# Seven buffers for modulation pieces, state evictions of the scan on ScalarE, and more turns between a solve and its product

## The chip, the cores and the metric

The kernel runs on one core of one Trainium2 chip. The metric is the device time of one execution in microseconds; it is given as the median of several runs. A trace of one profiled execution belongs to it.

In the views, PE is TensorE (PEld its weight loads), DVE is VectorE, ACT is ScalarE, POOL is GpSimd and SP the SyncE queue. A name such as `L99` is line 99 of the kernel. All operations that go through the helper class `Paced` carry its line, L49, so they are told apart by the names of their tiles.

## The reference

The kernel computes one inference step of a hybrid decoder layer in float32, for a prompt of 512 tokens and 8 single-token samples:

```python
mod = silu(c) @ w_ada + b_ada
sh1, sc1, gt1, sh2, sc2, gt2 = split(mod, 6)
h = modulate(rmsnorm(x, g_norm_mix), sh1, sc1)
proj = h @ w_in                      # q, k, v | columns of the RWKV-7 mixer
att = banded_attention(q, k, v)      # window 128, ALiBi, sinks
rw, S = rwkv7_mix(p_rwkv, S0)        # S_t = S diag(w) + (S a) b^T + v k^T ; y_t = S_t r_t
x = x + gt1 * (concat(att, rw) @ w_out)
h2 = modulate(rmsnorm(x, g_norm_ffn), sh2, sc2)
gate, up = split(h2 @ w_ffn_in, 2)
x = x + gt2 * ((silu(gate) * up) @ w_ffn_out)
y = rmsnorm(x, g_norm_final)
```

The model width is 2048, and there are 16 RWKV heads of 64. The modulation matrix `w_ada` is 2048 by 12288.

## The kernel before, in words

Each large matrix product is done with float32 weights split into a high and a low part. `unit` (L82 to L93) loads 128 x 512 weights into a `raw` buffer over the SP queue, ScalarE rounds them to `wh` (L89), and VectorE takes the rest as `wl` (L92). `mm3` (L95) multiplies with three products of two halves of the tokens (260 columns each), so one unit of four k-steps is 24 matmuls. There are three buffers each of `raw`, `wh` and `wl`.

After the modulation of the first norm, the stage this change bears on runs: `rwkv_phase` (L483). TensorE computes the projection tiles of `w_in` (`pm`, L99). Beside them run generators, the background jobs: `pump` (called once per k-step, six projection matmuls) advances each job that is due by one turn, that is up to its next `yield`. The jobs are:

- `ada_gen` (L308): the remaining modulation columns. 64 groups of four pieces of `w_ada` are loaded by SP into four tiles of the tag `ar` (L315 to L317), and 16 small matmuls per group (L322) sum them into the PSUM tile `ada`. The tag `ar` has 5 buffers. It also serves `adar` (results of a column group), `sp` (attention projections on their way to DRAM, L468) and, in the FFN, `s3` (L1499).
- For each of eight head pairs: `rwkv_prep1`, `rwkv_prep2` and `rwkv_rest` (L707). `rwkv_rest` first solves 32 x 32 triangular systems on VectorE, in 31 steps of a product (`stmp`, L721) and a sum (`Tt`, L724). The solution goes through DRAM to be laid out again: four DMAs `TTd<-Tt` from POOL and SP (L731), then one DMA `Td<-TTd` from POOL (L732). VectorE copies `Td` into `TT`. After one turn TensorE multiplies `TT` with `L3` into `pu` (two products; `L3` prints as `L`), and ScalarE copies `pu` back.
- The scan of the pair follows, 16 steps, each a chain across engines: TensorE forms `psc<-Z,L`; ScalarE copies the result to `Z` (two copies of 32 x 64); TensorE forms `psc<-Z,LS`; VectorE multiplies the result by the decay column `PC` and writes it as the state of the next step into `Z` (two `tensor_scalar` of 64 x 64, L777). The last step writes to a piece of `L3` instead, for the output. The next step's `psc<-Z,L` waits for this.

The order of instructions on an engine is not the order of the code. The tile framework takes the instructions in the order of the code as priority, and at each point gives an engine the first of them that is ready by the framework's own estimate of durations. An instruction that isn't ready by that estimate is thus passed by later ones. Each engine then executes its queue strictly in the order so found, and waits where the estimate was too early. An SP or POOL DMA whose buffer isn't free holds up all later DMAs of its queue.

After the stage come attention, the output projection, the FFN (`ffn_in`, `ffn_out`) and the last norm. In `ffn_in` POOL issues DMAs that add to a tile in SBUF (L1500, L1503), one of them to `s3`.

Of the kernel before, what the change touches and what calls it, by code (L numbers as in the profile page):

```python
# [7 lines left out]
F32 = mybir.dt.float32  # L8
F32R = mybir.dt.float32r
AF = mybir.ActivationFunctionType  # L10
ALU = mybir.AluOpType
# [3 lines left out]
P = 128  # L15
# [48 lines left out]
class Kern:  # L64
# [194 lines left out]

    def ada_finish(self, f0, n, ps):  # L260
        nc = self.px
        res = self.w.tile([P, 512], F32, tag="ar", bufs=5, name=self.nm("adar"))
        nc.scalar.copy(res[:, :n * 128], ps[:, :n * 128])
        yield
        p2 = self.aux("adT")
        for f in range(n):
            nc.tensor.matmul(p2[:, f * 16:f * 16 + 9], res[:, f * 128:(f + 1) * 128], self.sel, start=True, stop=True)
        nc.vector.tensor_tensor(
            self.mod[:, f0:f0 + n, :],
            p2[:, :n * 16].rearrange("p (f t) -> p f t", f=n)[:, :, :9],  # L270
            self.par[:, P_BA + f0:P_BA + f0 + n].unsqueeze(2).broadcast_to([P, n, 9]),
            ALU.add,
        )
# [34 lines left out]
    def ada_gen(self):  # L308
        nc = self.px
        for c in (GT1, SH2, SC2, GT2):  # L310
            for q in range(4):
                ci = c // 4 + q
                ps = self.hold("ada")
                for k0 in range(0, KD, 4):
                    raws = [self.w.tile([P, 512], F32, tag="ar", bufs=5, name=self.nm("ar")) for _ in range(4)]  # L315
                    for k, raw in enumerate(raws, k0):
                        self.nc.sync.dma_start(raw, self.I["w_ada2"][ci - 8, k])  # L317
                    self.done_at += 2.5
                    yield
                    for k, raw in enumerate(raws, k0):  # L320
                        for j in range(4):
                            self.nc.tensor.matmul(  # L322
                                ps[32 * j:32 * j + 32, 0:128], self.cT[:, k, :], raw[:, j * 128:(j + 1) * 128],
                                start=k == 0, stop=k == KD - 1, tile_position=(0, 32 * j), skip_group_check=True,
                            )
                    self.spent(self.nc.tensor, 0.8)
                    yield
                    yield
                res = self.w.tile([P, 512], F32, tag="ar", bufs=5, name=self.nm("adar"))[:, 0:128]
                nc.scalar.copy(res, ps[:, 0:128])  # L330
                yield
                p2 = self.aux("adT")
                nc.tensor.transpose(p2[:, 0:128], res, self.ident)
                nc.vector.tensor_tensor(
                    self.mod[:, 4 * ci:4 * ci + 4, :], p2[:, 0:128].rearrange("p (f t) -> p f t", f=4)[:, :, 0:9],
                    self.par[:, P_BA + 4 * ci:P_BA + 4 * ci + 4].unsqueeze(2).broadcast_to([P, 4, 9]), ALU.add)
# [41 lines left out]
    def startup(self):  # L378
        nc, I = self.nc, self.I
        xs = self.x_tiles()  # L380
        c = self.w.tile([P, 512], F32, tag="ar", bufs=5, name=self.nm("cr"))[:, 0:144]
        nc.sync.dma_start(c, I["c"].rearrange("p k t -> p (k t)"))
        k = 0
        for t, n in xs:
            nc.sync.dma_start(t, I["x"][:, k:k + n])
            k += n
        xk = [t[:, i] for t, n in xs for i in range(n)]
        nc.vector.memset(self.cT[:, :, 9:32], 0.0)
        nc.scalar.activation(self.cT[:, :, 0:9], c.rearrange("p (k t) -> p k t", t=9), AF.Silu)
        nc.scalar.activation(c[:, 0:2], self.cT[:, 0, 0:2], AF.Square)  # L390
        nc.scalar.activation(c[:, 2:4], c[:, 0:2], AF.Sqrt)
        ps = self.ps_m.tile([P, 2, 512], F32, tag="m", name="ssq1")
        for k in range(0, KD, 2):
            sq = [self.t520(t) for t in (("tC", "tD"), ("tA", "tB"))[k // 2 % 2]]
            nc.scalar.activation(sq[0], xk[k], AF.Square)
            if k % 4:
                nc.vector.tensor_tensor(sq[1], xk[k + 1], xk[k + 1], ALU.mult)
            else:
                nc.scalar.activation(sq[1], xk[k + 1], AF.Square)
            nc.vector.tensor_tensor(sq[0], sq[0], sq[1], ALU.add)  # L400
            for h in range(2):
                nc.tensor.matmul(ps[:, h, :HB], self.ones, sq[0][:, h], start=k == 0, stop=k == KD - 2)
        rstd = self.rstd_of(self.t520("tF"), ps)
        self.pcs, self.ring, self.used = {}, [], set()
        head = []
        for idx in (I_WA, I_G0, I_G1, 8, 0):
            src, m = self.w_in_src(idx)
            head.append((src, m, self.new_pc(idx)[:m, 1:513], self.SC[:m, idx]))
        self.hk = 0
        self.start(self.seq(self.h_parts(xk, rstd), self.ada_gen()))  # L410
        for k0, k1 in ((0, 2), (2, 4), (4, 8), (8, 12), (12, 14), (14, 16)):
            while self.hk < k1:
                self.pump()
            for tile_ in head:
                self.part_tile(*tile_, k0, k1)
# [44 lines left out]
    def filler(self):  # L460

        if not self.spills:
            self.pump()
            return
        idx, dram, scols = self.spills.pop(0)
        nc = self.nc
        ps = self.main_tile(self.I["w_in"][idx], self.hH, self.hL)
        t = self.w.tile([P, 512], F32, tag="ar", bufs=5, name=self.nm("sp"))  # L468
        nc.scalar.copy(t.rearrange("p (h t) -> p h t", h=2), ps[:, :, 0:256])
        nc.vector.tensor_copy(scols, ps[:, :, 256:260])  # L470
        nc.sync.dma_start(dram, t)
# [235 lines left out]
    def rwkv_rest(self, d):  # L707
        nc, I, rc = self.px, self.I, self.rc
        hp, L3, PC = (d[n] for n in ("hp", "L3", "PC"))
# [25 lines left out]
        for c4 in range(4):  # L735
            ro = slice(32 * c4, 32 * c4 + 32)
            nc.vector.tensor_copy(TT[ro, :, 32 * c4:32 * c4 + 32], Td[ro])
        yield
        for e in range(2):
            pu = self.aux("pu")  # L740
            for cq in range(4):
# [19 lines left out]
        for c in range(16):  # L761
            ps = self.aux_c(hp % 2)
            for e, o in ((0, 96), (1, 64)):
                nc.tensor.matmul(ps[o:o + 32, 0:64], L3[:, e, c // 4, (c % 4) * 32:(c % 4) * 32 + 32], Z[:, c, e],
                                 start=True, stop=True, skip_group_check=True, tile_position=(0, o))
            for e, o in ((0, 96), (1, 64)):
                nc.scalar.copy(Z[96:128, c, e], ps[o:o + 32, 0:64])
            self.done_at = self.now() + 1.2
            yield
            dst = Z[0:64, c + 1] if c < 15 else SF  # L770
            for e in range(2):
                ro = slice(64 * e, 64 * e + 64)
                nc.tensor.matmul(ps[ro, 64:128], LS[:, e, c, :], Z[:, c, e], start=True, stop=True, skip_group_check=True,
                                 tile_position=(0, 64 * e))
            for e in range(2):
                ro = slice(64 * e, 64 * e + 64)
                nc.vector.tensor_scalar(dst[:, e], ps[ro, 64:128], PC[ro, c:c + 1], None, ALU.mult)  # L777
            self.done_at = self.now() + 1.2
            yield
        nc.gpsimd.dma_start(self.O["wkvp"][:, hp], SF)  # L780
# [633 lines left out]
    def ffn_in(self, st):  # L1414
# [3 lines left out]
        tc, nc, I = self.tc, self.nc, self.I  # L1418
# [9 lines left out]
        sp = self.fpb.enter_context(tc.tile_pool(name="strw", bufs=1))  # L1428
# [5 lines left out]
        def load(ht, row, col, g, tag="sr"):  # L1434
            pool, n = (self.w, 3) if tag == "raw" else (sp, 6)
            if tag in places:
                pool, (tag, n) = self.xp, tag
            t = pool.tile([P, 512], F32, tag=tag, bufs=n, name=self.nm(tag))
            nc.sync.dma_start(t, src(ht, row, col, g))
            return t  # L1440
# [31 lines left out]
        for ht in range(early):  # L1472
            ps = mt("pm")
# [13 lines left out]
        for i, ht in enumerate(order):  # L1487
# [7 lines left out]
            for g in range(2):  # L1495
                a11, a21 = load(ht, 0, 0, g), load(ht, 1, 0, g, places[(2 * i + g) % 4])
                a22 = load(ht, 1, 1, g, "raw")
                a12 = load(ht, 0, 1, g)
                s3 = self.w.tile([P, 512], F32, tag="ar", bufs=5, name=self.nm("s3"))  # L1499
                nc.gpsimd.dma_start(a21, src(ht, 1, 1, g), accum_op=ALU.add)  # L1500
                if not (old and g):
                    nc.sync.dma_start(s3, src(ht, 0, 0, g))
# [251 lines left out]
```

## Time and profile before

| what | value |
|---|---|
| median of 3 runs | 2674.15 us (2666.03 to 2679.41) |
| profiled execution, its own time | 2681.19 us |
| its span, first to last instruction | 2679.4 us |
| mean granted TensorE clock | 0.976 |
| busy: PE, DVE, ACT, POOL | 2549.8, 1717.3, 1085.4, 380.0 us |
| `ada_gen`'s matmuls | 140.1 to 712.1 us |
| scans' matmuls `psc<-Z,L` | 267.8 to 871.0 us |
| FFN, about | 1230 to 2679 us |

The profiled execution took 7 us more than the median of the runs. A sum of stalls is made against it and then carried to the median as a difference. TensorE is busy nearly all the time, so what counts is its idle time and what ended it; idle time of the other engines matters only where TensorE waits for them.

### The profile page before, as it was taken

The page shows a single profiled execution, that of the slowest core. Times are in us where ns is not written, and L with a number is a line of the kernel's source. Part 1 is how long each engine was busy: PE and PEld are TensorE (multiplying, and loading weights), DVE is VectorE, ACT ScalarE, POOL GpSimd, SP SyncE. Part 2 cuts the span into 40 slices and gives each one's busy share as a digit, 9 for nine tenths or more (in the row PEclk, how much of TensorE's full clock was granted, in tenths as well). Part 3 has the DMA queues.
Part 4 walks back from the last instruction along what each step waited for, and adds up shares of the span by engine and source line. Part 5 has one row for each costly group of instructions (what it writes and reads, how often), then busy time and mean ns, then how long its engine had stood idle before and what let it go on. Part 6 is the DMA issues. An engine that isn't in the chain of part 4 may idle for free. (4 is left out here: it accounts for less than half of the span.)

```text
span 2679.4 us, 59146 instructions
## 1 busy us (share of the span) xinstructions
PE 2549.8 (95%) x23373; PEld 2367.4 (88%) x23373; DVE 1717.3 (64%) x3883; ACT 1085.4 (41%) x2155; POOL 380.0 (14%) x532
## 2 busy tenths in 40 slices
PE   7898999999999899998999999999999999999997
PEld 4587877778788898898999999999999999999997
DVE  5466656677656744568877777777777763444456
ACT  3133335344333323547544444444444432222225
POOL 0011111121111120011111121121121100000003
PEclk9998999999999997999999999999999999999999
DMA  9865564655423474445677777777787562343333
GB/s 339 294 197 181 172 198 151 189 164 187 132 86 106 165 231 141 120 143 180 186 206 182 211 207 194 195 204 196 186 219 199 133 206 91 123 127 97 119 103 111
DMA packets 241702, 460.21 MB, mean 172 GB/s; under 512 B 32352, under 2 KB 44560, under 8 KB 241392
## 3 DMA queue, kind: packets, MB, share of 16 engines
q1 hardware_dynamic: 206160, 377.22, 43.1%
q0 software_dynamic: 34624, 78.16, 13.5%
q8 instruction: 183, 3.00, 0.5%
q10 hardware_dynamic: 640, 1.05, 0.1%
q14 instruction: 95, 0.78, 0.1%
HBM read 421.73 MB, written 35.59 MB: 171 GB/s over the span
## 5 line engine op out<-in xcount | busy, mean ns | idle before, releaser
L89 ACT CAST wh<-raw 128x512 fp32r<-128x512 f32 (+2 forms) x410 | 247.0, 606 | 544.9 <-PE pf L99 281.1
L92 DVE TENSOR_TENSOR wl<-raw,wh 128x512 fp32r<-128x512 f32 (+2 forms) x410 | 283.9, 695 | 211.0 <-ACT wh L89 206.7
L99 PE MATMUL pf<-go,wh 128*128 128x260 f32 x2560 | 414.1, 281 | 0.0
L99 PEld LDWEIGHTS pf<-go,wh 128*128 128x128 f32 x2560 | 353.9, 188 | 0.1
L1282 ACT CAST wh<-sr 128x512 fp32r<-128x512 f32 x320 | 198.1, 621 | 261.0 <-PE pm L1453 235.1
L99 PE MATMUL pm<-hH,wh 128*128 128x260 f32 (+1 forms) x1248 | 290.9, 311 | 8.6 <-ACT wh L89 7.5
L99 PE MATMUL pm<-hH,wl 128*128 128x260 f32 (+1 forms) x1248 | 267.0, 293 | 12.1 <-DVE wl L92 12.0
L1283 DVE TENSOR_TENSOR wl<-sr,wh 128x512 fp32r<-128x512 f32 x320 | 220.3, 689 | 83.1 <-ACT wh L1282 76.1
L99 PE MATMUL pf<-go,wl 128*128 128x260 f32 x1280 | 267.7, 282 | 0.0
L99 PE MATMUL pm<-hL,wh 128*128 128x260 f32 (+1 forms) x1248 | 267.7, 293 | 0.0
L1453 PE MATMUL pm<-xT,wh 128*128 128x260 f32 x1408 | 263.6, 286 | 2.9 <-DVE pc L1530 2.5
L1453 PE MATMUL pm<-T,wh 128*128 128x260 f32 x1408 | 257.6, 283 | 0.0
L99 PEld LDWEIGHTS pm<-hH,wh 128*128 128x128 f32 (+1 forms) x1248 | 198.6, 192 | 46.6 <-issue 22.9
L1453 PEld LDWEIGHTS pm<-xT,wh 128*128 128x128 f32 x1408 | 217.2, 189 | 9.5 <-DVE pc L1530 4.6
L99 PEld LDWEIGHTS pm<-hH,wl 128*128 128x128 f32 (+1 forms) x1248 | 197.9, 192 | 23.1 <-DVE wl L92 15.5
L1453 PEld LDWEIGHTS pm<-T,wh 128*128 128x128 f32 x1408 | 216.9, 188 | 0.0
L1453 PE MATMUL pm<-B0H,wl 128*128 128x260 f32 x704 | 200.8, 286 | 8.6 <-DVE wl L1283 8.4
L99 PEld LDWEIGHTS pm<-hL,wh 128*128 128x128 f32 (+1 forms) x1248 | 198.7, 192 | 7.6 <-issue 3.9
L1453 PE MATMUL pm<-B0H,wh 128*128 128x260 f32 x704 | 200.2, 284 | 2.7 <-DVE acct L1219 1.7
L99 PEld LDWEIGHTS pf<-go,wl 128*128 128x128 f32 x1280 | 200.9, 188 | 0.0
L1453 PE MATMUL pm<-B0L,wh 128*128 128x260 f32 x704 | 198.9, 283 | 0.0
L1453 PE MATMUL pm<-T,wl 128*128 128x260 f32 x704 | 198.7, 282 | 0.0
(426 smaller groups left out, 5254.0 us busy)
## 6 DMA issues: line engine op xcount, KB each, us to landing
ar<-in_w_ada SPq DMA_DIRECT2D x256, 256.0 KB, 3.9
sr<-in_w_fi SPq DMA_DIRECT2D x176, 256.0 KB, 4.3
raw<-in_w_fo SPq DMA_DIRECT2D x176, 256.0 KB, 2.6
raw<-in_w_in SPq DMA_DIRECT2D x144, 256.0 KB, 3.8
araw<-in_w_ada SPq DMA_DIRECT2D x64, 512.0 KB, 6.3
raw<-in_w_fi SPq DMA_DIRECT2D x120, 256.0 KB, 4.4
s<-in_w_fi SPq DMA_DIRECT2D x80, 256.0 KB, 4.8
s<-in_w_fi POOLq DMA_DIRECT2D x80, 256.0 KB, 5.5
```

What stands on the lines that cost most here:

```text
L89: nc.scalar.copy(wh[:, :n], raw[:, :n])
L92: nc.vector.tensor_tensor(wl[:, :n], raw[:, :n], wh[:, :n].bitcast(F32), ALU.subtract)
L99: nc.tensor.matmul(ps[:m, bank, :HB], w, a[:, k, h, :], start=first and i == 0, stop=last and i == 2, skip_group_check=True,)
L1282: nc.scalar.copy(H, src)
L1283: nc.vector.tensor_tensor(L, src, H.bitcast(F32), ALU.subtract)
L1453: nc.tensor.matmul(ps[:, :HB], x[:, s], y, start=g == k == i == 0, stop=g == 1 and k == 3 and i == 2, skip_group_check=True)
```

## The change

- The tag `ar` gets 7 buffers in place of 5, at all five places that name it. The 4 KiB per partition come out of the scratch in which POOL's DMA descriptors are kept, which goes from 8192 to 4096 bytes per partition.
- The two evictions at the end of each scan step (256 in all) become `activation` with the function Copy and the column `PC` as scale, on ScalarE.
- `rwkv_rest` yields four times in place of once between the copies into `TT` and the products `pu`.

```diff
-        res = self.w.tile([P, 512], F32, tag="ar", bufs=5, name=self.nm("adar"))
+        res = self.w.tile([P, 512], F32, tag="ar", bufs=7, name=self.nm("adar"))
...
-                    raws = [self.w.tile([P, 512], F32, tag="ar", bufs=5, name=self.nm("ar")) for _ in range(4)]
+                    raws = [self.w.tile([P, 512], F32, tag="ar", bufs=7, name=self.nm("ar")) for _ in range(4)]
...
             nc.vector.tensor_copy(TT[ro, :, 32 * c4:32 * c4 + 32], Td[ro])
-        yield
+        for _ in range(4):
+            yield
         for e in range(2):
             pu = self.aux("pu")
...
             for e in range(2):
                 ro = slice(64 * e, 64 * e + 64)
-                nc.vector.tensor_scalar(dst[:, e], ps[ro, 64:128], PC[ro, c:c + 1], None, ALU.mult)
+                nc.scalar.activation(dst[:, e], ps[ro, 64:128], AF.Copy, scale=PC[ro, c:c + 1])
...
-                s3 = self.w.tile([P, 512], F32, tag="ar", bufs=5, name=self.nm("s3"))
+                s3 = self.w.tile([P, 512], F32, tag="ar", bufs=7, name=self.nm("s3"))
...
-    nc = bacc.Bacc("TRN2", target_bir_lowering=False, num_devices=1, dynamic_dma_scratch_size=8192)
+    nc = bacc.Bacc("TRN2", target_bir_lowering=False, num_devices=1, dynamic_dma_scratch_size=4096)
```

The line numbers after the `yield` are one higher in the changed kernel. The order of the queues changes as follows.

TensorE's queue at the first pair's product `pu`, before. `pm` are projection tiles, `wh` and `wl` the weights of a unit, `ada` the modulation sums from pieces `ar`, `pV` the first product behind `pu`:

```order
L99 MATMUL pm_2755<-hH,wl_2968 128x260 x2
L322 MATMUL ada_2861<-ar_2957,cT 32x128 x4
L322 MATMUL ada_2861<-ar_2958,cT 32x128 x4
L322 MATMUL ada_2861<-ar_2959,cT 32x128 x4
L322 MATMUL ada_2861<-ar_2960,cT 32x128 x4
L99 MATMUL pm_2755<-hH,wh_2967 128x260 x2
L99 MATMUL pm_2755<-hL,wh_2967 128x260 x2
L99 MATMUL pm_2755<-hH,wl_2968 128x260 x2
L99 MATMUL pm_3030<-hH,wh_3033 128x260 x2
L49 MATMUL pu_2904<-TT,L_288_1790 128x128 x4
L49 MATMUL pu_2939<-TT,L_288_1790 128x128 x4
L49 MATMUL pV_2985<-cst,V_2259 128x128 x4
```

The same place in the changed kernel:

```order
L99 MATMUL pm_2755<-hH,wh_2953 128x260 x2
L99 MATMUL pm_2755<-hL,wh_2953 128x260 x2
L99 MATMUL pm_2755<-hH,wl_2954 128x260 x2
L322 MATMUL ada_2861<-ar_2969,cT 32x128 x4
L322 MATMUL ada_2861<-ar_2970,cT 32x128 x4
L322 MATMUL ada_2861<-ar_2971,cT 32x128 x4
L322 MATMUL ada_2861<-ar_2972,cT 32x128 x4
L99 MATMUL pm_3028<-hH,wh_3031 128x260
L49 MATMUL pu_2945<-TT,L_288_1790 128x128 x4
L49 MATMUL pu_2977<-TT,L_288_1790 128x128 x4
L49 MATMUL pV_3014<-cst,V_2259 128x128 x4
```

The product stands at the same weight unit's start as before, one projection matmul into it in place of two; ahead of it there are 961 projection matmuls in the whole queue, and 962 before. The modulation group moved to stand right in front of it. Numbers of tiles grow in the order of the code: `pu_2904` is written ahead of the units 2967 and 3033 and stands behind them, so it is held back by the framework's estimate of when `TT` is there, and not by the turns.

VectorE's queue during the solve of the second pair, before. `stmp` and `Tt` are the solve, `tB` the cumulative sums of the next pair's preparation, `Z<-psc,PC` the evictions of the first pair's scan:

```order
L721 TENSOR_TENSOR stmp_3585<-Tt,As 128x70
L49 SCALAR_TENSOR_TENSOR tB_3633<-scan,tA_3628 128x128
L724 TENSOR_TENSOR Tt<-Tt,stmp_3585 128x5x14
L49 SCALAR_TENSOR_TENSOR tB_3633<-scan,tA_3628 128x128
L721 TENSOR_TENSOR stmp_3600<-Tt,As 128x65
L49 TENSOR_SCALAR Z_1738<-psc,PC_1791 64x64
L724 TENSOR_TENSOR Tt<-Tt,stmp_3600 128x5x13
L49 TENSOR_SCALAR Z_1738<-psc,PC_1791 64x64
L721 TENSOR_TENSOR stmp_3603<-Tt,As 128x60
```

ScalarE's queue at the same place of the changed kernel. `tA`, `tD`, `tH` and `tC` are the next pair's preparation, `wh` a weight cast, `ACT_TABLE_LOAD` the change to another set of functions:

```order
L49 COPY Z_1738<-psc 32x64 x2
L49 ACTIVATE Z_1738<-psc,PC_1791 64x64 x2
L49 ACT_TABLE_LOAD
L49 ACTIVATE tA_3624<-pw_3618,der 128x512
L49 ACTIVATE tD_3626<-pa_3621,der 128x512
L49 COPY Z_1738<-psc 32x64 x2
L49 ACTIVATE tH_3778<-tD_3626,der 128x512
L89 CAST wh_3828<-raw_3826 128x512
L49 ACTIVATE Z_1738<-psc,PC_1791 64x64 x2
L49 ACTIVATE tC_3774<-tB_3629 128x512
```

The evictions left the solve and stand among ScalarE's preparation, casts and function loads. ScalarE's queue has 30 function loads in place of 28. All else that the kernel issues is the same in number and shape. TensorE's queue is the same from the end of the sample's mixer on (the last row that differs stands ahead of attention). In the FFN, SP and POOL issue the loads and additions for `s3` up to two pieces sooner.

More of the change, by code (lines that the diff above doesn't have):

```diff
@@ L328, in ada_gen @@
                     yield
-                res = self.w.tile([P, 512], F32, tag="ar", bufs=5, name=self.nm("adar"))[:, 0:128]
+                res = self.w.tile([P, 512], F32, tag="ar", bufs=7, name=self.nm("adar"))[:, 0:128]
                 nc.scalar.copy(res, ps[:, 0:128])
@@ L380, in startup @@
         xs = self.x_tiles()
-        c = self.w.tile([P, 512], F32, tag="ar", bufs=5, name=self.nm("cr"))[:, 0:144]
+        c = self.w.tile([P, 512], F32, tag="ar", bufs=7, name=self.nm("cr"))[:, 0:144]
         nc.sync.dma_start(c, I["c"].rearrange("p k t -> p (k t)"))
@@ L467, in filler @@
         ps = self.main_tile(self.I["w_in"][idx], self.hH, self.hL)
-        t = self.w.tile([P, 512], F32, tag="ar", bufs=5, name=self.nm("sp"))
+        t = self.w.tile([P, 512], F32, tag="ar", bufs=7, name=self.nm("sp"))
         nc.scalar.copy(t.rearrange("p (h t) -> p h t", h=2), ps[:, :, 0:256])
```

## The prediction

> **What bounds the kernel now.** I read the busy times and clock by stage first, then who waits for whom in the stage of the scans, then the timeline at the waits. The stages, with the header of that view:
>
> ```profile
> core 0: us, PE busy (x) PEld busy (x) DVE busy (x) ACT busy (x) POOL busy (x), PEclk, DMA share, GB/s
> 140.00:260.00 120.00, 106.39 (x1201) 94.23 (x1199) 75.67 (x180) 45.87 (x84) 22.31 (x29) 0.96 0.64 201
> 260.00:880.00 620.00, 582.62 (x6821) 488.10 (x6822) 410.77 (x1138) 255.54 (x612) 106.83 (x161) 0.96 0.49 152
> 1230.00:2155.00 925.00, 908.92 (x7418) 896.21 (x7417) 698.63 (x1219) 446.68 (x764) 171.28 (x222) 1.00 0.72 195
> ```
>
> TensorE is the bound in every stage. From 140 to 880 us it idles 51.0 us (13.6 + 37.4) of 740; in the FFN's first part 16 of 925. The change's code runs in the first two rows, so only those 51 us can be won, and whatever the change does there counts only through TensorE's queue. Who ended that idle time, from 140 to 890 us (total, times, longest; then the same three as TensorE's weight loads show them):
>
> ```profile
> PE psc L49 <- DVE Z L49: 16.4, 21, 2.2
> PE pu L49 <- DVE TT L49: 14.9, 7, 4.1
> PE ada L322 <- DMA ar<-in_w_ada: 9.4, 13, 4.3
> PE pm L99 <- DVE wl L92: 4.2, 4, 2.1
> PE psc L49 <- ACT Z L49: 2.8, 5, 1.8
> PE pm L99 <- ACT wh L89: 1.0, 1, 1.0
> ```
>
> ```profile
> PEld psc L49 <- DVE Z L49: 22.5, 28, 2.4
> PEld ada L322 <- DMA ar<-in_w_ada: 14.6, 18, 4.6
> ```
>
> Three waits make 40.7 us, and each edit aims at one: evictions on VectorE, the solution `TT`, the modulation pieces. Ends of matmuls are modelled, so a short stall is partly covered in the matmul rows and fully seen in the weight loads; the true loss lies between the two views. 40.7 us is 1.5% of the time: the most that could go if nothing new came. About 0.5% (13 us) is what a measurement of this kernel can tell from no change.
>
> **The change part by part.**
>
> *Evictions to ScalarE.* What they cost on VectorE, the chain's twin on ScalarE, and the nearest rows for the new instruction (one with a column as scale, one without, and one twice as long):
>
> ```profile
> L49 DVE TENSOR_SCALAR Z<-psc,PC 64x64 f32<-64x64 f32 x240 | 67.7, 282 | 74.6 <-PE psc L49 66.0 <-ACT adar L49 3.7
> L49 ACT COPY Z<-psc 32x64 f32<-32x64 f32 x256 | 52.3, 204 | 138.8 <-PE psc L49 135.3 <-DVE tA L49 0.5
> L1612 ACT ACTIVATE x<-x,par 128x260 f32<-128x260 f32 x32 | 14.9, 506 | 0.5
> L1225 ACT ACTIVATE sqh<-x 128x260 f32<-128x260 f32 x8 | 3.3, 415 | 1.4 <-DVE x L1220 1.4
> L1225 ACT ACTIVATE sqh<-x 128x520 f32<-128x520 f32 x28 | 17.8, 637 | 16.1 <-DVE x L1220 14.3 <-POOL acc L1247 1.1 <-issue 0.4
> ```
>
> From 520 to 260 columns an ACTIVATE loses 222 ns, 0.85 ns a column; 64 columns with a scale column are thus 506 - 196 x 0.85 = 339 ns, against 282 (bounds: the 204 of the copy, the 506). Each eviction alone gets 57 ns dearer: by that alone the 21 waiting steps, two evictions each, would cost 2.4 us more. The Trainium skill says this too ("ScalarE: Activation LUTs", Rules for kernel authors: multiplications belong on VectorE); by that rule alone the term would be +2.4 us and not a gain. I don't follow it, since the price is not what TensorE waits for; the place in the queue is. At the first large wait VectorE did this:
>
> ```profile
> 309.86 0.26 DVE L721 TENSOR_TENSOR stmp<-Tt,As 128x65 f32<-128x65 f32 x1
> 310.15 0.28 DVE L49 TENSOR_SCALAR Z<-psc,PC 64x64 f32<-64x64 f32 x1
> 310.35 1.03 DVE L724 TENSOR_TENSOR Tt<-Tt,stmp 128x65 f32<-128x65 f32 x1
> 311.41 0.29 DVE L49 TENSOR_SCALAR Z<-psc,PC 64x64 f32<-64x64 f32 x1
> ```
>
> ```profile
> 311.76 0.30 PE L49 MATMUL psc<-Z,L 128*32 128x64 f32 x4 [1.98 <-DVE Z L49]
> ```
>
> Two evictions took 1.55 us because a solve step of 1.03 us stood between them (the step's first half took 0.26). On ScalarE the other half of the same chain, the copies, stands in the queue under like conditions for as many steps, and costs TensorE 2.8 us, not 16.4. Load speaks for it too: 256 x 282 ns = 72 us leave VectorE (410.8 to 339 of 620, 55%), and 256 x 339 = 87 come to ScalarE (255.5 to 342, 55%). TensorE's queue also gives more room: of 126 steps, those with under 12 projection matmuls between a state's product `psc<-Z,LS` and the next `psc<-Z,L` fall from 76 to 54, and between `psc<-Z,L` and `psc<-Z,LS` those under 6 from 47 to 21. I take 19.5 us as the loss now (middle of 16.4 and 22.5) and 3.5 as what stays (2.8 and a little for the longer instruction): **-16 us**; bounds 0 and -22.5.
>
> *Seven buffers.* SP's queue is held by the pieces' buffers:
>
> ```profile
> SPq L317 <- PE ada L322: 137.6, 91, 7.8
> ```
>
> Of a group's four loads, three had to wait for the group before (five buffers), now one. Loads so run ahead, and the waits of 9.4 to 14.6 us (say 12) should nearly vanish. But the largest, 5.3 us, stands in front of the first pair's `pu`:
>
> ```profile
> 252.39 0.45 PE L322 MATMUL ada<-ar,cT 128*32 128x128 f32 x8 [4.35 <-DMA ar<-in_w_ada]
> 253.11 0.66 PE L322 MATMUL ada<-ar,cT 128*32 128x128 f32 x8 [0.28 <-DMA ar<-in_w_ada]
> 254.45 0.65 PE L322 MATMUL ada<-ar,cT 128*32 128x128 f32 x8 [0.69 <-DMA ar<-in_w_ada]
> ...
> 260.92 3.75 PE L49 MATMUL pu<-TT,L 128*128 128x128 f32 x16 [3.78 <-DVE TT L49]
> ```
>
> What TensorE saves at 252 it waits longer at 261, since `TT` comes by DMAs that don't depend on it (next part). That leaves 12 - 5.3 = 6.7, of which I take **-5 us** (bounds 0 and -14.6). In the FFN the two buffers let `s3` load sooner; TensorE loses almost nothing there to weights (8.4 us, all on `wl`), and `raw` with 3 and `sr` with 6 buffers still limit the run-ahead, so 0.
>
> ```profile
> PE pm L1453 <- DVE wl L1283: 8.4, 19, 1.5
> ```
>
> *Smaller descriptor scratch.* No row shows POOL waiting for room in it. POOL's DMAs are behind one another by the waits of their data; I take 0, with bounds of 0 and the FFN's 8.4 us once more.
>
> *More turns before `pu`.* What `TT` waits for in the first and the last pair:
>
> ```profile
> 247.63 0.17 DVE L724 TENSOR_TENSOR Tt<-Tt,stmp 128x8 f32<-128x8 f32 x1
> 248.10 1.18 POOL L731 DMA_DIRECT2D TTd<-Tt  x2 [3.70 <-DVE Tt L724]
> 252.34 0.92 POOL L732 DMA_DIRECT2D Td<-TTd  x1 [3.06 <-DMA TTd<-Tt]
> 259.88 0.89 DVE L49 COPY TT<-Td 32x256 f32<-32x256 f32 x3
> ...
> 786.22 0.17 DVE L724 TENSOR_TENSOR Tt<-Tt,stmp 128x8 f32<-128x8 f32 x1
> 795.67 1.18 DVE L49 COPY TT<-Td 32x256 f32<-32x256 f32 x4 [3.65 <-DMA Td<-TTd]
> 797.00 2.05 PE L49 MATMUL pu<-TT,L 128*128 128x128 f32 x8 [4.06 <-DVE TT L49]
> ```
>
> From the last solve step to the product pass 13.3 and 10.8 us, nearly all of it two DMA round trips that the change leaves alone. Three more turns are 18 projection matmuls, at 0.12 us each (the FFN row: 7418 in 908.9 us) 2.2 us: they would take most of the 14.9 us away if the product moved back by them. It doesn't. The order shows `pu` held by the framework's estimate and not by the turns; the first pair's stands after 961 projection matmuls in place of 962. Over the eight pairs I counted the projection matmuls from the first use of the last `wl` ahead of the solve's end in VectorE's queue to `pu`: 184 before, 94 after. By this the products stand nearer to their solves, on average by 11 matmuls or 1.4 us. Bounds: -14.9 if the lighter VectorE makes up for all, and 8 x 1.4 = +11. I take **+2.5 us**.
>
> *New waits.* ScalarE's queue is stopped by others, and evictions now stand behind that:
>
> ```profile
> ACT Z L49 <- PE psc L49: 135.3, 88, 5.5
> ACT L L49 <- PE pu L49: 43.8, 14, 7.8
> ACT wh L89 <- DMA raw<-in_w_in: 34.2, 10, 6.9
> ```
>
> Weight casts that wait behind evictions may starve a projection tile; three buffers cover this now (5.2 us on `wl` and `wh`). Two more function loads are off the path. **+2.5 us**, bounds 0 and +10.
>
> Sum: -16 - 5 + 2.5 + 2.5 = **-16 us**; 2681.2 becomes 2665 in a profiled execution, the median 2674 becomes **2658**.
>
> **The rivals.**
>
> *The product's wait goes too* (0.15). VectorE, 72 us lighter, ends each solve sooner against TensorE, and the 14.9 us go along with the 5.3 that I carried over. The clock adds to it; it falls with these stalls:
>
> ```profile
> 250.00:260.00 10.00, 3.79 (x32) 2.36 (x32) 3.36 (x7) 1.17 (x3) 2.79 (x8) 0.63 0.88 273
> 260.00:270.00 10.00, 9.08 (x65) 8.74 (x69) 7.07 (x12) 4.51 (x9) 2.00 (x4) 0.68 0.10 36
> ```
>
> Two slices of 10 us at 0.63 and 0.68 lose 3.7 and 3.2 us of full clock, of which I count 5. -16 - 5 - 15 - 5 + 2.5 is -38: 2636. Against it: the DMA round trips stay. The Trainium skill names such a clock loss after an idle window of about 3.4 us ("TensorE: Matmul & The Clock Gate", Part 1). By that rule the trace agrees: 0.63 and 0.68 around stalls of 4.35 and 3.78 us.
>
> *No net change* (0.22). The products stand nearer by the full 11 us and the evictions save half: -8 - 5 + 11 + 2.5 = 0: 2674. For it: the counts above.
>
> *Slower: ScalarE's queue becomes the gate of the scan* (0.11). Evictions there wait as they did on VectorE (0 won), the copies behind them wait as the evictions do (2.8 to 11, +8), late casts cost +10, `pu` +2.5, pieces -5: +15, 2689. It decides from where TensorE's waits on ScalarE's `Z` pass the 19.2 us that both `Z` waits take now. Against it: 55% load.
>
> **How the numbers follow.** My forecast has 0.52, with 2648 to 2668 as its own spread. The bound for faster is 2661, so about 0.35 of it counts as faster and 0.17 as the same. With the rivals: faster 0.50, same 0.39, slower 0.11. The range 2638 to 2680 leaves out the slower rival and most of the best.
>
> **What would show it.** In the changed profile, TensorE's wait on ScalarE's `Z` should be 3 to 8 us and none on VectorE's; on `ar` under 4; on `TT` 13 to 24, with over 6 at the first pair; idle from 140 to 880 us near 35. If the wait on `TT` is under 8, my reading of the turns is wrong; if ScalarE's `Z` takes over 19, that of the evictions.

## The result, and the profile after

The changed kernel takes **2658.78 us** (median of 8 runs, 2651.25 to 2665.93), the kernel before 2672.65 beside it (8 runs, 2666.03 to 2681.11). The ratio is **0.994, 95% interval 0.9923 to 0.9957**: 0.4 to 0.8% faster. The forecast was 2658. The profiled execution took 2657.65 us (span 2655.8) against 2681.19 before, but the profiled execution of before lies 8.5 us above its median and this one 1 below. So of the 23.5 us between the two profiles only the 14 of the medians need a cause.

Busy time in the two rows that the change's code runs in, in the columns of the first view of the prediction:

```profile
140.00:260.00 120.00, 109.21 (x1178) 99.32 (x1177) 76.68 (x178) 45.99 (x84) 23.58 (x31) 0.91 0.61 198
260.00:880.00 620.00, 586.59 (x6908) 498.59 (x6908) 360.70 (x899) 339.47 (x877) 120.59 (x165) 0.96 0.49 157
```

VectorE is at 361 us of 620, ScalarE at 339 (forecast 339 and 342). TensorE idles 44.2 us from 140 to 880 (10.8 + 33.4), 51.0 before; I had named 35. Who ended that idle time, 140 to 890 us, first for TensorE's matmuls, then for its weight loads:

```profile
PE pu L49 <- DVE TT L49: 17.2, 6, 5.0
PE psc L49 <- ACT Z L49: 8.8, 13, 1.8
PE ada L322 <- DMA ar<-in_w_ada: 8.0, 4, 5.7
PE pt L49 <- DVE RR L49: 5.6, 1, 5.6
PE adT L49 <- DVE RR L49: 2.0, 2, 1.5
PE pm L99 <- DVE wl L92: 1.2, 2, 0.9
```

```profile
PEld psc L49 <- ACT Z L49: 15.1, 31, 2.1
...
PEld ada L322 <- DMA ar<-in_w_ada: 9.4, 5, 5.9
```

The waits on `Z` fell from 19.2 us to 8.8, all of them now on ScalarE. The wait of `pu` rose from 14.9 to 17.2. At the first pair it is 3.0 us, where I had named over 6. The wait on the pieces hardly moved, 9.4 to 8.0, and one stall of 5.7 us is most of it. New is one wait of 5.6 us on the last pair's groupnorm (`RR`), which VectorE does between wide instructions of the samples' work that now run beside it.

To compare stages of like work I take the time from TensorE's first `ada` matmul to its first `ptx` (the product behind the projections): 827.9 us before, 808.4 after. I call this **the stage**. Of the 19.5 us, 13.4 are idle time of TensorE (58.2 to 44.8) and 6.1 its busy time (769.7 to 763.6).

The evictions on ScalarE, beside the copies, over the whole execution:

```profile
L49 ACT ACTIVATE Z<-psc,PC 64x64 f32<-64x64 f32 x240 | 74.2, 309 | 82.7 <-PE psc L49 79.7 <-issue 0.5
L49 ACT COPY Z<-psc 32x64 f32<-32x64 f32 x256 | 52.1, 204 | 54.9 <-PE psc L49 51.6
```

309 ns each, against 282 on VectorE and an estimate of 339. The copies idle 55 us ahead of them where it was 139: the two halves of the chain now meet in one queue.

The waits on `Z` that are left are explained by what stands in that queue. ScalarE and TensorE of the changed kernel around the largest:

```profile
548.16 0.63 ACT L49 ACTIVATE tA<-tA 128x512 f32<-128x512 f32 x1 [2.58 <-POOL tA L49]
548.69 0.61 ACT L49 ACTIVATE tB<-tB 128x512 f32<-128x512 f32 x1
549.33 0.42 ACT L49 COPY Z<-psc 32x64 f32<-32x64 f32 x2
549.77 0.62 ACT L89 CAST wh<-raw 128x512 fp32r<-128x512 f32 x1
550.41 1.28 ACT L49 ACT_TABLE_LOAD   x1
551.70 0.60 ACT L49 ACTIVATE tF<-pn 128x512 f32<-128x512 f32 x1
552.20 0.62 ACT L49 ACTIVATE Z<-psc,PC 64x64 f32<-64x64 f32 x2
```

```profile
549.80 0.34 PE L49 MATMUL psc<-Z,LS 128*64 128x64 f32 x4 [1.80 <-ACT Z L49]
...
552.87 0.31 PE L49 MATMUL psc<-Z,L 128*32 128x64 f32 x4 [1.10 <-ACT Z L49]
```

The copies stood behind `tA` and `tB`, and `tA` had waited 2.58 us for GpSimd: 1.80 us lost. The evictions then stood behind a function load of 1.28 us and `tF`: 1.10 us lost. Of the five waits of 0.9 us or more in this stage three stand behind a function load and two behind `tA` and `tB`; together they are 6.0 of the 8.8 us.

The first pair's `pu`, SP's queue and then TensorE's, changed kernel:

```profile
243.30 1.33 SPq L731 DMA_DIRECT2D TTd<-Tt  x2
244.72 0.56 SPq L87 DMA_DIRECT2D raw<-in_w_in  x1
245.38 1.81 SPq L317 DMA_DIRECT2D ar<-in_w_ada  x4
```

```profile
250.27 0.65 PE L322 MATMUL ada<-ar,cT 128*32 128x128 f32 x8 [5.67 <-DMA ar<-in_w_ada]
250.86 0.59 PE L99 MATMUL pm<-hH,wh 128*128 128x260 f32 x1
254.46 3.75 PE L49 MATMUL pu<-TT,L 128*128 128x128 f32 x16 [3.02 <-DVE TT L49]
```

The pieces whose lateness costs 5.67 us stand in SP's queue behind `TTd`, which waits for the end of the solve. No buffer is short there, so two more don't help.

### The profile page after: what moved, and what is told of

Read it like the earlier page. It is cut to its first block, busy times and chain, and to the rows that moved or that the text cites. A ratio compares the mean times of both kernels' runs of the same rounds, so it can differ in the third digit from the quotient of the medians.

```text
span 2655.8 us, 58969 instructions
## 1 busy us (share of the span) xinstructions
PE 2539.9 (96%) x23373; PEld 2368.0 (89%) x23373; DVE 1648.6 (62%) x3627; ACT 1166.6 (44%) x2413; POOL 384.7 (14%) x532
## 3 DMA queue, kind: packets, MB, share of 16 engines
q0 software_dynamic: 34624, 78.16, 13.4%
## 5 line engine op out<-in xcount | busy, mean ns | idle before, releaser
L99 PE MATMUL pm<-hL,wh 128*128 128x260 f32 (+1 forms) x1248 | 260.4, 289 | 0.0
L99 PEld LDWEIGHTS pm<-hH,wl 128*128 128x128 f32 (+1 forms) x1248 | 196.1, 190 | 13.8 <-DVE wl L92 7.1
```

What stands on the lines that cost most here:

```text
L99: nc.tensor.matmul(ps[:m, bank, :HB], w, a[:, k, h, :], start=first and i == 0, stop=last and i == 2, skip_group_check=True,)
```

## The experiments

The theory after this look: the evictions carry the gain; buffers and turns do next to nothing. The rivals: buffers or turns carry it, or the parts need each other. The first four kernels do one part each. All ratios are to the kernel before, run on the same chip in the same session; it had a median of 2679 us in the first four, 2677 in the others.

**Evictions alone** (the kernel before with this edit):

```diff
-                nc.vector.tensor_scalar(dst[:, e], ps[ro, 64:128], PC[ro, c:c + 1], None, ALU.mult)
+                nc.scalar.activation(dst[:, e], ps[ro, 64:128], AF.Copy, scale=PC[ro, c:c + 1])
```

> Only the evictions on ScalarE; five buffers, the old scratch, one turn. Theory (the evictions carry the gain): TensorE's waits on Z fall from 19.2 us to 7 to 10, all of them on ScalarE's Z; the wait of pu on TT stays at 13 to 18 (the products stand after 158 projection matmuls from their solves over the eight pairs, 184 before), the wait on the pieces at 8 to 10; 10 to 14 us under the kernel before. Rival 1 (the gain is made by buffers and turns): within 4 us of the kernel before. Rival 2 (the evictions only pay together with the turns): half of the gain, 5 to 8 us.

Measured: 2653.95 us, ratio 0.9900 (0.9872 to 0.9929). TensorE's waits, 140 to 890 us:

```profile
PE pu L49 <- DVE TT L49: 10.7, 5, 3.5
PE psc L49 <- ACT Z L49: 10.0, 14, 2.5
PE ada L322 <- DMA ar<-in_w_ada: 6.3, 5, 4.4
```

25 us by the medians, 27 by the ratio: by the medians more than the whole change brings, and more than the theory named. The waits on `Z` fell by 9 us as expected. `pu`, pieces and weights wait 9 us less too, and the groupnorm costs 5 us more than before. So the waits give about 14 us; over the whole stage TensorE idles 19.5 us less (58.2 to 38.7) and is busy 5.8 us less, which together is the 25.3 us by which the stage is shorter. The same edit also gave the scan more room in TensorE's order, which could be the cause instead; 20 turns alone, below, speak to that.

**Buffers alone** (`bufs=5` to `7` at the tag `ar`, scratch 8192 to 4096):

> Only the seven buffers and the smaller scratch; evictions on VectorE, one turn. My forecast of this term was 5 us less. What the changed kernel's trace makes of it: its wait on the pieces was still 8.0 us of 9.4, 5.7 of them where SP's queue stands behind the TTd transfers of the first pair, so now 0 to 2 us less; the wait on the pieces 7 to 9.4, on Z 17 to 20. Rival (the buffers carry the gain): 8 to 14 us less.

Measured: 2687.63 us, ratio 1.0034 (1.0017 to 1.0051): **slower**, which neither had. TensorE's waits, and VectorE's wait for the transfer behind `TT`:

```profile
PE pu L49 <- DVE TT L49: 27.0, 8, 6.4
PE psc L49 <- DVE Z L49: 17.1, 22, 2.2
PE ada L322 <- DMA ar<-in_w_ada: 5.9, 3, 3.9
```

```profile
DVE TT L49 <- DMA Td<-TTd: 33.4, 7, 10.3
```

The pieces do wait less (9.4 to 5.9), but `pu` waits 12 us longer. TensorE gets to `pu` sooner and `TT` does not.

**Turns alone** (`yield` to four of them):

> Only four turns in place of one before pu. Theory (the product is placed by the framework's estimate, the turns hardly count): the products stand after 157 projection matmuls from their solves in place of 184, so 0 to 3 us more, the wait of pu on TT 13 to 20. Rival (the turns cover the round trip): the wait of pu falls under 6 us, 8 to 15 us less.

Measured: 2665.50 us, ratio 0.9962 (0.9944 to 0.9980): **faster**, by 10 us by the ratio, against the theory.

```profile
PE psc L49 <- DVE Z L49: 16.8, 16, 2.7
PE ada L322 <- DMA ar<-in_w_ada: 9.3, 5, 6.3
PE pu L49 <- DVE TT L49: 7.5, 4, 2.5
```

The wait on `TT` was halved, to neither theory's number; the time is the rival's.

**Scratch alone** (4096, five buffers):

> Only the descriptor scratch, 4096 in place of 8192, with nothing in its room. Theory: no change, within 3 us, and the same waits of TensorE as in the kernel before, so that its profile shows how far one execution differs from another. Rival (POOL's transfers stop for room): 4 to 10 us more, with longer waits of POOL's and TensorE's work on its transfers.

Measured: 2677.47 us, ratio 0.9997 (0.9981 to 1.0014). The scratch does nothing, so the cost of the buffers is the buffers'. TensorE's order is that of the kernel before, so this profile also shows how far one execution differs from another: stage 831.7 us (827.9), and

```profile
PE psc L49 <- DVE Z L49: 15.7, 20, 2.2
PE pu L49 <- DVE TT L49: 15.1, 7, 3.8
PE ada L322 <- DMA ar<-in_w_ada: 8.8, 11, 4.3
```

Between these two executions of one order each of the rows shown moves by under 1 us, the waits on `Z` together by 1.5 (19.2 to 17.7) and the stage by 3.8. The 7 and 12 us by which the wait on `TT` moved with the turns and with the buffers are well beyond that, so I put them down to the edits.

**The pairs.** The changed kernel without its extra turns, and without its buffers:

> Evictions on ScalarE, seven buffers and the smaller scratch, one turn: the changed kernel without its extra turns. If the parts add up (evictions alone 25 us less, buffers alone 8 us more), 17 us less than the kernel before, with a wait of pu on TT of 15 to 25 us, above the 10.7 us with five buffers. Rival (the buffers cost only where the slow evictions are): 23 to 28 us less, a wait of pu near 11. Rival 2 (buffers and evictions get in each other's way and the turns repair it): less than 12 us less.

> Evictions on ScalarE and four turns; five buffers and the old scratch: the changed kernel without its buffers. If the parts add up (25 and 14 less by the medians, 10 by the ratio), 35 us less than the kernel before, with waits of 6 us or less on TT and 8 to 10 on ScalarE's Z. Rival (both win the same wait of pu, which is 10.7 us with the evictions alone): 25 to 29 us less, the wait of pu on TT at 7 to 11.

Measured: evictions and buffers 2656.57 us, 0.9922 (0.9907 to 0.9937); evictions and turns 2653.20 us, 0.9914 (0.9892 to 0.9936). The first lies between its theory and its rival (21 us less by the medians, the wait of `pu` at 15.0), the second next to its rival (24 us less, 8.1): evictions and turns win in part the same wait. All kernels with one or four turns side by side; the stage and the waits are from one execution each, the waits TensorE's in its matmul rows, in us:

| kernel | ratio | stage, us | on Z | on TT | on pieces |
|---|---|---|---|---|---|
| before | 1 | 827.9 | 19.2 | 14.9 | 9.4 |
| buffers | 1.0034 | 843.0 | 17.7 | 27.0 | 5.9 |
| turns | 0.9962 | 818.9 | 18.8 | 7.5 | 9.3 |
| evictions | 0.9900 | 802.6 | 10.0 | 10.7 | 6.3 |
| evictions, turns | 0.9914 | 811.9 | 9.3 | 8.1 | 9.2 |
| evictions, buffers | 0.9922 | 807.6 | 11.0 | 15.0 | 4.5 |
| all (the change) | 0.9940 | 808.4 | 8.8 | 17.2 | 8.0 |

Each comparison with and without buffers has them cost: 0.34% alone, 0.22% beside the evictions, 0.26% beside evictions and turns. Only the first is resolved by its own interval, but in each the wait on `TT` rises by more (12.1, 4.3 and 9.1 us) than the pieces give (3.5, 1.8, 1.2). The turns bring 0.38% alone and nothing that can be told from zero on top of the evictions (0.9900 to 0.9914) or of evictions and buffers (0.9922 to 0.9940). The parts don't add up: the single ratios would give 0.990 + 0.0034 - 0.0038, that is 0.9896, and 0.9940 was measured.

**`TTd` off SP's queue** (the changed kernel with this edit):

```diff
-            q2[g % 2].dma_start(self.TTd[hp][:, g:32:4], Tt[32 * g:32 * g + 32])
+            q2[0].dma_start(self.TTd[hp][:, g:32:4], Tt[32 * g:32 * g + 32])
```

> The changed kernel with all four TTd transfers of a solve on GpSimd's queue, none on SP's. Theory: at the first pair the pieces wait because SP's queue stands behind TTd until the solve ends; without it the wait of 5.7 us on the pieces goes (8.0 to under 3 in all), but pu waits for TT by about as much longer, and two more transfers of 0.6 us stand on GpSimd ahead of Td: within 6 us of the changed kernel, on the slower side. Rival (what TensorE saves there is kept): 4 to 6 us less.

Measured: 2657.17 us, 0.9934 (0.9916 to 0.9953), the same as the changed kernel.

```profile
PE pu L49 <- DVE TT L49: 25.7, 7, 6.1
PE psc L49 <- ACT Z L49: 10.9, 19, 1.8
PE ada L322 <- DMA ar<-in_w_ada: 3.6, 2, 3.1
```

The pieces' wait is halved, and `pu` takes it all over and 4 us more, since two transfers more stand ahead of `Td` on GpSimd (`Td` is issued 6.8 us after the last solve step on average, 4.5 in the changed kernel; from that step to `pu` pass 13.8 us, 11.6 there). What is saved in front of `pu` without moving `TT` is not kept. This holds here and with the buffers.

**20 turns** (the changed kernel with `range(20)`):

> The changed kernel with 20 turns in place of 4 between the copies of TT and pu. The products then stand after 622 projection matmuls from their solves over the eight pairs, 94 with four turns: 66 more for each, 7.9 us at 0.12 us. Theory (the product is placed nearer than the round trip of 10 to 12 us): the wait of 17.2 us on TT falls under 4 us, 10 to 15 us less than the changed kernel's 2659, if the scan's end, 178 matmuls later, stays before the projections' end. Rival (the wait moves on: the later product starves the scan, whose next steps and the groupnorm come late): the wait of pu gone and the time within 5 us of the changed kernel, with new waits on Z, on ScalarE's L or ahead of ptx.

Measured: **2634.29 us, ratio 0.9848 (0.9831 to 0.9865)**, 1.5% under the kernel before and 0.9% under the changed one.

```profile
PE psc L49 <- ACT Z L49: 11.0, 13, 2.6
PE ada L322 <- DMA ar<-in_w_ada: 9.0, 9, 2.7
```

The wait on `TT` is gone; those on `Z` and on the pieces grew by 3 us in all, and the one of 5.6 us on `RR` is gone too. From 140 to 880 us the changed kernel and this one:

```profile
140.00:880.00 740.00, 695.80 (x8084) 597.91 (x8083) 437.37 (x1076) 385.46 (x960) 144.17 (x196) 0.95 0.51 164
```

```profile
140.00:880.00 740.00, 714.60 (x8344) 619.11 (x8344) 447.50 (x1097) 393.12 (x976) 139.45 (x196) 0.98 0.53 169
```

Idle falls from 44.2 to 25.4 us, and the granted clock rises from 0.95 to 0.98. The stage takes 782.0 us, 26 less. The same two kernels over the stage, which has the same matmuls in both:

```profile
135.80:944.20 808.40, 763.61 (x8660) 664.09 (x8660) 466.63 (x1142) 407.33 (x999) 149.14 (x205) 0.96 0.53 168
```

```profile
136.60:918.50 781.90, 753.17 (x8659) 656.29 (x8659) 466.22 (x1142) 405.06 (x997) 144.73 (x206) 0.98 0.55 174
```

Of the 26 us, 16 are idle time (44.8 to 28.7) and 10 are busy time, in which the same matmuls took less at a granted clock of 0.98 in place of 0.96.

**20 turns with other company**: without the buffers, and with neither evictions nor buffers.

> Evictions on ScalarE and 20 turns, with five buffers and the old scratch: the 20-turn kernel without its buffers. Theory (seven buffers cost because pieces loaded ahead lengthen the transfer of Td, on which pu waits): with pu's wait covered that cost is hidden, so within 4 us of the 20-turn kernel with seven buffers (43 us less than the kernel before), no wait on TT. Rival (the buffers cost in another place, as in slower weight loads): 6 to 9 us below it, 50 us less than the kernel before.

> Only 20 turns, evictions on VectorE, five buffers, old scratch. Theory (pu's wait of 15 us and the fall of the clock behind it are a cost of their own): the wait on TT under 3 us, the waits on Z near 19 us as before; 18 to 25 us less than the kernel before. Rival (the evictions had to move first, since with them on VectorE the solve ends late and the wait moves to Z or to TT): within 8 us of the kernel before.

Measured: evictions and 20 turns 2639.92 us, 0.9859 (0.9843 to 0.9874); 20 turns alone 2650.57 us, 0.9914 (0.9899 to 0.9929). TensorE's waits with 20 turns alone:

```profile
PE psc L49 <- DVE Z L49: 18.5, 23, 1.9
PE ada L322 <- DMA ar<-in_w_ada: 6.0, 7, 2.5
PE pu L49 <- DVE TT L49: 2.6, 2, 1.7
```

Twenty turns alone bring 0.86%, 23 us, more than the whole change. With `pu` covered the buffers show no cost (0.9859 without, 0.9848 with them, with intervals that overlap). This fits a cost that goes through `pu`'s wait. And with `pu` covered the evictions are seen by themselves: 0.9914 to 0.9859, **15 us**, for waits on `Z` that fall from 19.5 to 7.9.

The kernel with 20 turns alone also answers whether the place in the queue or the room in TensorE's order ends the waits on `Z`. Counted in the traces, the steps with under 12 projection matmuls between `psc<-Z,LS` and the next `psc<-Z,L` are 75 before, 60 with the evictions alone and 61 with 20 turns alone; those with under 6 from `psc<-Z,L` to `psc<-Z,LS` are 47, 25 and 22. Thus 20 turns alone have about the same room as the evictions alone, with the evictions still on VectorE, and the waits on `Z` stayed at 19.5, where the evictions alone had 10.0. So the room by itself does not end these waits, and the queue remains as the cause.

**30 turns** (the changed kernel with `range(30)`):

> The changed kernel with 30 turns in place of 4. The products stand after 1162 projection matmuls from their solves over the eight pairs (622 with 20 turns), the last at 3462 in place of 3102. Theory (20 turns already cover the round trip, more only makes the scan end later): no wait on TT, nothing more won, and up to 20 us slower than with 20 turns, since 360 matmuls more, 43 us, go by before the last scan, which then has fewer projections beside it. Rival (more cover still helps): 3 to 8 us under the 20 turns.

Measured: 2640.31 us, 0.9874 (0.9857 to 0.9892), 6 us above 20 turns, with intervals that overlap by a little. No wait on `TT` is left here either. TensorE's waits from 880 to 1000 us, and the busy times of a part of it:

```profile
PE ptx L49 <- DMA vf<-kvd: 10.0, 2, 8.1
PE pt L49 <- DVE RR L49: 4.5, 1, 4.5
```

```profile
880.00:940.00 60.00, 39.96 (x306) 33.01 (x307) 28.77 (x85) 22.38 (x60) 12.32 (x17) 0.69 0.82 247
```

The last scan's product starts at 887.4 us, behind the last projection (876.8); with 20 turns it was 857.3 against 889.2. TensorE then waits 8.1 us for a load that attention needs, idles 20 of 60 us, and the clock is at 0.69. In this execution, cover beyond the round trip is paid for at the end; that the kernel is slower than with 20 turns is not shown, since the intervals overlap.

**Two extra loads** (the kernel before with the smaller scratch; the loads go where the two buffers would lie):

```diff
+        for k in range(2):
+            dm = self.w.tile([P, 512], F32, tag="dm", bufs=2, name=self.nm("dm"))
+            self.nc.sync.dma_start(dm, self.I["w_ada2"][hp, k])
         q2[0].dma_start(Td, self.TTd[hp].rearrange("(q c) s t -> (c s) q t", c=4))
```

> The kernel before with the smaller scratch and, in its room, two extra loads of 256 KB on SP's queue behind the TTd transfers of each solve, which nobody reads; evictions, buffers and turns as before. It asks whether loads that run ahead cost by lengthening Td. Theory: Td's landing goes from 4.0 us to 5 or more, pu's wait on TT from 15 to 20 to 30 us, 5 to 15 us slower than the kernel before. Rival (Td isn't held by loads on another queue; the seven buffers cost by the order): Td stays at 4.0 to 4.3 us, pu's wait within 3 us, the time within 3 us.

Measured: 2679.03 us, 1.0011 (0.9996 to 1.0027). When the loads and the transfers `Td` were issued (first and last start in us), and then the landing of `Td` in the kernel with the buffers alone (median from issue to landing at the end of the row):

```profile
L734 SPq DMA_DIRECT2D dm<-in_w_ada x16: 327/423/430, 130.3 to 198.5; - x16
L735 POOL DMA_DIRECT2D Td<-TTd x8: 917/922/996, 251.8 to 789.2; - x8
```

```profile
Td<-TTd POOLq DMA_DIRECT2D x8, 128.0 KB, 5.2
```

The edit did not do what it was meant to do. The extra loads depend on nothing, so the framework issued all 16 of them by 198.5 us, before the first `Td` at 251.8: none ran beside a `Td`. That `Td` stayed at 4.2 us (4.0 before) and `pu`'s wait at 16.4 therefore decides nothing between theory and rival; the run shows only that 4 MB of loads in that earlier place cost nothing that can be measured.

The traces lean to the theory. In the 3 us behind the issue of a `Td`, the other DMA queues moved 191 GB/s on average in the kernel before and 249 with the buffers alone, and `Td` landed after 4.4 and 5.2 us on average. Over all 14 kernels, the 32 of 112 such transfers with under 150 GB/s beside them landed after 3.6 us on average, the 58 with over 250 after 5.4. This is an association and not a proof: many of the quiet ones belong to the last two pairs, where the loads of `w_ada` have ended. The Trainium skill ("DMA: Bandwidth & Descriptors", Queues, rings and completion order) says that each DMA engine goes round between the queues that have work. By that, loads of SP in flight would take turns from GpSimd's transfer; no run here shows it alone. A longer `Td` is in any case the smaller part: from the last solve step to `pu` 11.2 us passed with the buffers alone on average, against 10.6 before, 5 us over the eight pairs, where the wait on `TT` rose by 12.

## Why the forecast was right, and where its steps were wrong

The sum, -16 us, met the 14 measured. That moving the evictions carries the gain is shown. That the sum came out so close is luck in part: run alone, the evictions bring 25 to 27 us and not 16, two other terms had the wrong sign (buffers +9 for -5, turns -10 for +2.5), and the single ratios add up to 28 us, about twice what the parts bring together. TensorE's idle time from 140 to 880 us was 44.2 us where I had named 35, the waits on the pieces 8.0 where I had named under 4, and those on `Z` 8.8, just above the 3 to 8.

- **Evictions, -16.** Shown. Where `pu`'s wait is covered they bring 15 us, with 11.6 us less of waits on `Z`; beside four turns alone 13 (0.9962 to 0.9914), with one turn 27, and 30 beside the buffers (1.0034 to 0.9922). The higher numbers contain waits of `pu` that grow shorter too. 8.8 us of waits stay, not 3.5. I had put the function loads "off the path"; three of the five large waits that are left stand behind one. The step that said place in the queue counts more than price (309 against 282 ns) held. The Trainium skill's rule that multiplications belong on VectorE ("ScalarE: Activation LUTs", Rules for kernel authors) has the price right in sign, and these runs the other way in time.
- **Seven buffers, -5.** Wrong: +9 alone, and in no pairing with one or four turns a gain. I saw that a stall in front of `pu` comes back at `pu`, but applied it to one stall of 5.3 us and kept the other 6.7. The runs show it for more than that one: the pieces gave 3.5 us and `pu` took 12, since VectorE's solve and two transfers, not TensorE, say when `TT` is there. That `pu` took more than was saved is measured and only partly explained (the longer `Td`, about 5 us); the rest stays open. That the stall of 5.7 us stayed has another reason, which stood in the order and which I didn't look for: its loads are queued behind `TTd`. I had named under 4 us for the pieces; they are at 8.0.
- **Scratch, 0.** Right (0.9997).
- **More turns, +2.5.** In the change as a whole the wait on `TT` rose by 2.3 us, but not for the reason given. I held that turns don't place the product, and counted projection matmuls from the solve's end (184 to 94). Run alone, four turns give a count of 157, nearer than before, and the wait fell from 14.9 to 7.5. The count starts at the place in VectorE's queue where a solve ends, and that place has no fixed time on TensorE. What raised the wait in the change is the buffers: 8.1 without them, 17.2 with them. Turns place the product well when there are enough of them: 20 move it by 66 matmuls a pair.
- **New waits, +2.5.** Near in size (3.3 in sum), by luck, since it arose in another place: the casts' waits fell (`wl` 4.2 to 1.2, `wh` 1.0 to 0.2) where I had them grow, and `RR` cost 5.6 once (0.5 before) and 2.0 for `adT`.

Of the rivals, ScalarE as the gate is excluded by 8.8 us on `Z`, where 19.2 was the point, and no net change by the interval of the ratio, which ends at 0.9957. The first rival, `pu`'s wait gone with its clock, was priced at 2636 us; the changed kernel didn't do it, but 20 turns do, at 2634. That the numbers meet is luck: the rival's sum has one term of 5 us for two that it names (the stall carried over and the clock), and with both it gives 2630. The clock belongs to its price all the same: of the 26 us by which 20 turns shorten the stage, 10 are busy time of the same matmuls.

## What to carry to other kernels

When an engine waits at a point whose operand comes at a time of its own (a solve and two transfers), what is saved ahead of that point was not kept in the two kernels that tried it; move the point back by the round trip, here 20 turns and not 4, and only then tune what stands ahead of it. A small instruction in a chain across engines belongs in the queue that has the fewest long instructions in its way, even where it costs more by itself; function loads count among the long ones. Run the parts of a change singly: here one part alone did at least as well as the whole, and one made the kernel slower.

## What the runs showed of the hardware

- A function load takes 1.28 us on ScalarE, and the next instruction starts at once: the cast ahead of it ended at 550.39, the load ran from 550.41, `tF` from 551.70. The Trainium skill ("ScalarE: Activation LUTs", What ACT_TABLE_LOAD costs) has the same 1283 ns but adds about 1380 ns of drain; no such time is seen here.
- A Copy of 64 x 64 from PSUM with a column as scale takes 309 ns on ScalarE, 282 on VectorE as a multiplication.
- Over 112 transfers of 128 KB on GpSimd's queue, those with under 150 GB/s on other queues in their first 3 us landed after 3.6 us on average, those with over 250 GB/s after 5.4. That the other traffic is the cause is not shown.
